# Reordering the start of a diffusion block: the conditions' loads first, weights ahead of w_ada, first products pass by pass

## The chip, the cores and the metric

The kernel runs on one core of a Trainium2 chip. The metric is the device time of one execution in microseconds; lower is better. An execution is some 1.7 us longer than its span, the time from the first to the last of the program's own instructions. Engines are named as in the profile: PE (TensorE), DVE (VectorE), ACT (ScalarE), POOL (GpSimd), SP (SyncE, which here issues the loads).

## What is computed

One block of a hybrid diffusion backbone over 512 latent tokens and 256 context tokens of 1024 features, in fp32. Cut to what bears on the change:

```
mod_lat = split(silu(c) @ w_ada + b_ada, 6)          # scale, shift, gate, twice
mod_ctx = split(silu(c_ctx) @ w_ada + b_ada, 6)
pl = project(modulate(rmsnorm(x, g_mix), sh1, sc1), w_in, w_dec_up, b_dec)
pc = project(modulate(rmsnorm(ctx, g_mix), sh1c, sc1c), w_in, w_dec_up, b_dec)
# project: h @ w_in gives q, k, v, g, dd (decay rank 16, two directions), conv and gate columns;
# dd @ w_dec_up + b_dec -> log decay
o_c, s_cf, s_cb = gla_bidir(context)                  # 4 heads, chunks of 64
o_l = gla_bidir(latent, from the context's states)
...                                                   # short convolution, gates, output projections,
                                                      # SwiGLU, final rmsnorm
```

## The kernel before

A matrix product of two fp32 operands is made from three passes: each operand is split into a rounded high part (fp32r) and the rest, and `mm3` (L153) issues high by high, high by low and low by high into one PSUM bank. A split is one cast on ACT (the high part) and one subtraction on DVE (the low part), `split` at L102 for all tiles.

The start of the program is what the change touches. Four loads bring the 512 latent tokens (`xt`, 128 tokens each), two small ones the conditions c and c_ctx (`c_rows`, 16 rows of 128), then come small vectors. PE turns `c_rows`, ACT takes the SiLU into `c2` and, with a second table, a square root `root`, and then the tokens in turn: `normed` squares and scales a token tile, `turn` transposes it into `xsT` (features on partitions).

The scale and shift of the mixer's input come from the first 2048 columns of w_ada in four parts (`p_` = 0 to 3) of two feature tiles each: `ada_load` issues eight loads of 256 KB a part, `ada_rows` makes 16 matmuls of them, DVE copies the row out (`adar`), `mod_cols` turns it into columns with eight small matmuls (`adac`) and two DVE steps (`modT`, `gs`), and `modulate(f)` makes feature tile f of `h`: ACT writes the high part, DVE scales `xsT` in place and subtracts. Beside each part goes one unit of the projection weights, `w0_load(p_)`: 256 rows of w_in with head 0's value columns, the 32 decay columns and head 0's key and query columns, 544 KB in four loads into one of three buffers `r_w`; `w0_split` splits a unit into `h_w` and `l_w`.

Then a loop over the eight feature tiles k: `gather_v` adds tile k's products to the values and decays of the four latent token tiles (`vo`, four banks, twelve matmuls), `gather_kq` to head 0's keys and queries (`ko`, `qo`, six matmuls). After the odd tiles 1, 3 and 5 the next part follows inside the loop: its w_ada rows, the key and query products of tile k-1, its columns, the first `modulate`, the weights' split, the second `modulate`. After tile 6 the context tokens (normalised after tile 5) are turned and split into `hc`; `head0_gather` then makes the context's products in the same way, and inside it, at k = 5, `ddt` transposes the latent decays (`st` into `ddT`) and `vps2` the late vectors. The context's own decays are turned a little later, behind four steps of the first g tile, and the decays' products `z` follow.

Order: from `pinned[0] = True` (L471) on each engine runs its instructions in the order of the program's text. All loads but those of w_dec_up (POOL) are issued by SP in the order of the text; a load waits there for its buffer, and each load uses one of eight semaphores in turn, so a ninth waits until the first of the eight has landed.

Of the kernel before, what the change touches and what calls it, by code (L numbers as in the profile page):

```python
# [9 lines left out]
F32R = mybir.dt.float32r  # L10
BF16 = mybir.dt.bfloat16
U8 = mybir.dt.uint8
AF = mybir.ActivationFunctionType
ALU = mybir.AluOpType
PSUM = bass.MemoryType.PSUM

P = 128
D = 1024
KT = D // P
T = 512  # L20
TC = 256
NT = T // P
# [24 lines left out]
def hybrid_block(ctx: ExitStack, tc: tile.TileContext, x, c, ctxt, c_ctx, w_ada, b_ada, g_mix, w_in,  # L47
# [8 lines left out]
    wp = ctx.enter_context(tc.tile_pool(name="wp", bufs=3))  # L56
# [8 lines left out]
    def u2(name, dt=F32, shape=(P, 512)):  # L65
        return up.tile(list(shape), dt, tag="u2", name=name, bufs=NU)
# [17 lines left out]
    def bank(name, shape=(P, 512)):  # L84
        return ps.tile(list(shape), F32, tag="ps", name=name, bufs=3)

    def gbank(name, shape=(P, 512)):
        return ps.tile(list(shape), F32, tag="pg", name=name, bufs=5)
# [15 lines left out]
    act_, dve = Pinned(nc.scalar), Pinned(nc.vector)  # L104

    def f32(ap):
        return ap.bitcast(F32)
# [35 lines left out]
    def pe_pin(ins):  # L143
        if pinned[0]:
            tc.keep_in_program_order(ins)

    def mm(*a, **k):
        pe_pin(nc.tensor.matmul(*a, **k))  # L148

    def tr(*a):  # L150
        pe_pin(nc.tensor.transpose(*a))

    def mm3(o, a, b, start, stop):  # L153
        mm(o, a[0], b[0], start=start, stop=False)
        mm(o, a[0], b[1], start=False, stop=False)
        mm(o, a[1], b[0], start=False, stop=stop)

    def rstd_of(ss, n, width, name):

        r = sm.tile([P, n], F32, tag=f"rs{n}", name=f"rs_{name}")  # L160
        act_.activation(r, ss, AF.Sqrt, bias=eps, scale=1.0 / width)
        dve.reciprocal(r, r)
        return r
# [4 lines left out]
    def token_load(i):  # L168
        if i < NT:
            xt = hp.tile([P, D], F32, tag="xt", name=f"xt{i}", bufs=4)  # L170
            nc.sync.dma_start(xt, x[i * P:(i + 1) * P, :])
        else:
            xt = wp.tile([P, D], F32, tag="raw", name=f"xt{i}", bufs=4)
            nc.sync.dma_start(xt, ctxt[(i - NT) * P:(i - NT + 1) * P, :])
        return xt

    xts = [token_load(i) for i in range(NT)]
    c_rows = cst.tile([16, P], F32, name="c_rows")
    nc.sync.dma_start(c_rows[0:8, :], c.rearrange("o (r f) -> (o r) f", f=P))
    nc.sync.dma_start(c_rows[8:16, :], c_ctx.rearrange("(r f) -> r f", f=P))  # L180

    ident = cst.tile([P, P], F32, name="ident")
    make_identity(nc, ident)
# [4 lines left out]
    def small_vectors(vs):  # L188
        for r0, src in vs:
            n = src.shape[1] // P  # L190
            for d in range(src.shape[0]):
                nc.sync.dma_start(vrow[r0 + d * n:r0 + (d + 1) * n, :P], src[d:d + 1, :].rearrange("o (r f) -> (o r) f", f=P))
# [27 lines left out]
    for d in range(2):  # L220
        t = cst.tile([P, NT, P], F32, name=f"TP{d}")
# [21 lines left out]
    xsT = hp.tile([P, KT, T], F32, name="xsT")  # L243

    def normed(i, xt):
        junk = u2(f"junk{i}", BF16, (P, D))
        ss = sm.tile([P, 1], F32, tag="ss", name=f"ss{i}")
        act_.activation(junk, xt, AF.Square, accum_out=ss)
        dve.tensor_scalar_mul(xt, xt, rstd_of(ss, 1, D, f"x{i}"))
# [8 lines left out]
    modT = cst.tile([P, KT, 2, 2], F32, name="modT")  # L258
    gs = cst.tile([P, KT, 2], F32, name="gs")

    def ada_load(p_):

        us = []
        src = w_ada[:, :2 * D].rearrange("(k p) (s f) -> p k s f", p=P, s=2)[:, :, :, p_ * 256:(p_ + 1) * 256]
        if p_ < 2:
            for k in range(0, KT, 2):
                if p_ == 0:
                    t = wp.tile([P, 2, 2, 256], F32, tag="raw", name=f"wa{p_}{k}", bufs=4)
                else:
                    t = hp.tile([P, 2, 2, 256], F32, tag="wa", name=f"wa{p_}{k}", bufs=4)  # L270
                for i in range(2):
                    nc.sync.dma_start(t[:, i], src[:, k + i])
                us += [t[:, i].rearrange("p s f -> p (s f)") for i in range(2)]
        else:
            for k in range(KT):
                t = (uh if p_ == 2 else uo)(f"wa{p_}{k}", F32, (P, 2, 256))
                nc.sync.dma_start(t, src[:, k])
                us.append(t.rearrange("p s f -> p (s f)"))
        return us

    def ada_rows(p_, us):

        rows = gbank(f"ada{p_}")
        for k in range(KT):
            g_ = 32 * (k % 4)
            mm(rows[g_:g_ + 32, :], cw[:, k, :], us[k], start=k < 4, stop=k >= KT - 4)
        rsb = u2(f"adar{p_}")
        dve.tensor_copy(rsb, rows)
        return rsb

    hhi, hlo = hbig("h")
    h = [(hhi[k // 4][:, k % 4, :], hlo[k // 4][:, k % 4, :]) for k in range(KT)]
    hc = []

    def mod_split(src, f, j, hi, lo):
        g_, sh = gs[:, f, j:j + 1], modT[:, f, 0, j:j + 1]
        act_.activation(hi, src, AF.Identity, scale=g_, bias=sh)
        dve.tensor_scalar(src, src, g_, sh, ALU.mult, ALU.add)
        dve.tensor_sub(lo, src, f32(hi))
# [13 lines left out]
    def modulate(f):  # L313
        mod_split(xsT[:, f, :], f, 0, *h[f])
# [34 lines left out]
    def run(steps):  # L349
        for _ in steps:  # L350
            pass
# [83 lines left out]
    NW = HV + 32  # L435

    def w0_load(p_):

        r = hp.tile([P, 2, NW + 256], F32, tag="wr", name=f"r_w0{p_}", bufs=3)
        for d0, c0, n in ((0, CV, HV), (HV, CD, 32), (NW, CK, P), (NW + P, CQ, P)):  # L440
            nc.sync.dma_start(r[:, :, d0:d0 + n], w_in[p_ * 256:(p_ + 1) * 256, c0:c0 + n].rearrange("(a p) b -> p a b", p=P))
        return r

    def w0_at(k, a, e):
        return tuple(w_[:, k % 2, a:e] for w_ in w0[k // 2])

    def gather_v(os, src, k):
        for i, o in enumerate(os):
            mm3(o[:, :NW], tuple(w_[:, i * P:(i + 1) * P] for w_ in src[k]), w0_at(k, 0, NW), k == 0, k == KT - 1)

    def gather(o, c0, src, k, n=T):
# [2 lines left out]
    w0 = []  # L454
# [6 lines left out]
    vo = [bank(f"v0_{NC_}")]  # L461

    wdu_ = wdu_load()
    was, wrs = [], []
    for p_ in range(4):
        was.append(ada_load(p_))
        wrs.append(w0_load(p_))
    small_vectors(((R_GH, g_head), (R_BD, b_dec[0]), (R_WC, w_conv[0])))
    xcs = [token_load(NT + i) for i in range(NC_)]
    lat = (xsT[:, :4, :], xsT[:, 4:, :])  # L470
# [14 lines left out]
    def w0_split(p_):  # L485
        w0.append(split_raw(wrs[p_], f"w0{p_}"))

    modulate(0)
    w0_split(0)
    modulate(1)  # L490
    wdu_split(*wdu_)
    vo += [(bank if i < 3 else gbank)(f"v0_{NC_ + i}") for i in range(1, NT)]
# [11 lines left out]
    for k in range(KT):  # L504
        p_ = k // 2 + 1
        more = k % 2 == 1 and p_ < 4
        gather_v(vo, h, k)
        if more:
            rsb = ada_rows(p_, was[p_])
            gather_kq(k - 1)  # L510
            mod_cols(p_, rsb)
            modulate(2 * p_)
            w0_split(p_)
            modulate(2 * p_ + 1)
            if p_ == 3:
                for i in range(NC_):
                    normed(NT + i, xcs[i])
        if k % 2 or k >= 6:
            gather_kq(k)
        if k == 6:  # L520
            xcT = [wp.tile([P, 4, TC], F32, tag="raw", name=f"xcT{i}", bufs=4) for i in range(2)]
            for i in range(NC_):
                turn(NT + i, xcs[i], xcT, i)
            for f in range(KT):
                mod_ctx(f)
# [12 lines left out]
    def head0_gather():  # L538
        for k in range(KT + 2):
            if k < KT:  # L540
                gather_v(vc, hc, k)
            if k >= 2:
                gather(kc, NW, hc, k - 2, TC)
            if k == 5:
                ddt(NC_, NC_ + NT)
                vps2 = gbank("vps2")
                tr(vps2[:, :R_N], vrow[:R_N, :P], ident[:R_N, :R_N])
                dve.tensor_copy(vec[:, 64:], vps2[:, 64:R_N])
# [370 lines left out]
    for pr in range(KT // 2):  # L919
# [3 lines left out]
        for j in range(2):  # L923
            o = proj(sl_, j, f"cc{pr}{j}")
            t = ux(f"cc{pr}{j}")
# [5 lines left out]
        for j in range(2):  # L931
            ct = 2 * pr + j
            o = proj(sl_, j, f"ch{pr}{j}")
            t = ux(f"u{ct}", F32, (P, ROWS, GW))
# [9 lines left out]
        for j in range(2):  # L944
            o = proj(sl_, j, f"cb{pr}{j}")
            t = ux(f"cbu{pr}{j}")
            nc.vector.tensor_mul(t, o, ucs[j].rearrange("p r w -> p (r w)"))
            hi, lo = ux(f"cuh{pr}{j}", F32R), ux(f"cul{pr}{j}", F32R)
# [13 lines left out]
    for pr in range(KT // 2):  # L962
        ada_tick()
        sl_ = Slab(w_conv_out, pr * 256, 256, f"co{pr}")
        for j in range(2):
            o = proj(sl_, j, f"yc{pr}{j}", rhs=cu)
            nc.vector.tensor_mul(mg[2 * pr + j], o, mg[2 * pr + j])
    oghl = []
    for i, t in enumerate(og):
        mk = uv if i < 3 else ux  # L970
        hi, lo = mk(f"ogh{i}", F32R), mk(f"ogl{i}", F32R)
# [3 lines left out]
    for pr in range(KT // 2):  # L975
        ada_tick()
        sl_ = Slab(w_gla_out, pr * 256, 256, f"go{pr}")
        for j in range(2):
            i = 2 * pr + j
            o = proj(sl_, j, f"yg{pr}{j}", rhs=oghl)  # L980
            t = ux(f"yg{pr}{j}")
            nc.vector.tensor_mul(t, o, sas[pr, j])
            nc.vector.tensor_add(t, t, mg[i])
            hi, lo = ux(f"meh{i}", F32R), ux(f"mel{i}", F32R)
# [105 lines left out]
    for t in range(NT):  # L1090
        o = mix(t, 1, sl_, steps_of(t))
# [12 lines left out]
    for pr in range(FT // 2):  # L1104
# [16 lines left out]
        for j in range(2):  # L1121
# [4 lines left out]
            hi, lo = mk(f"ah{pr}{j}", F32R), mk(f"al{pr}{j}", F32R)  # L1126
# [65 lines left out]
```

## Time and profile before

| what | us |
|---|---|
| three timed runs | 1028.50, 1027.01, 1028.37 |
| their median | 1028.37 |
| the profiled execution | 1028.95 |
| its span | 1027.2 |
| PE busy in it | 992.8 (97%), 5221 matmuls |
| DVE busy | 545.7 (53%) |
| ACT busy | 381.9 (37%) |
[...]
| loads | 114 MB from HBM |

A row of the view in order of time has the start and the duration of one or several equal instructions, the engine, the line, the operation, what it writes and reads, its shape and count; in square brackets how long the engine sat idle before it and what ended that. SPq is a load's issue. Matmuls are pipelined, so that a row of several is shorter than their sum, and the ends are modelled. PEld is the load of stationary weights, which overlaps the matmuls.

### The profile page before, as it was taken

What the parts mean: (1) busy time and instruction counts of PE and PEld (TensorE: products, weight loads), DVE (VectorE), ACT (ScalarE), POOL (GpSimd) and SP (SyncE); (2) the same over time, 40 slices, a digit from 0 to 9 for tenths busy, and PEclk for the clock granted to TensorE, in tenths of its full rate; (3) what the DMA queues carried; (4) which work ended last, traced back from release to release, by engine and by line L of the source; (5) the groups of instructions that cost most, each with busy time, mean ns of one, the idle gap of its engine ahead of it and who ended that gap; (6) DMA issues with size and microseconds to landing.
All of it is one profiled execution on the core that took longest, in us unless ns stands there. A gap on an engine that the chain in (4) does not pass through costs nothing.

```text
span 1027.2 us, 12874 instructions
## 1 busy us (share of the span) xinstructions
PE 992.8 (97%) x5221; PEld 829.6 (81%) x5221; DVE 545.7 (53%) x845; ACT 381.9 (37%) x602; POOL 6.3 (1%) x18
## 2 busy tenths in 40 slices
PE   4888999999999999999999999999999999999997
PEld 2667889888788888888888888888888888888886
DVE  4456868777656587678534434743343333322423
ACT  4146464647635322233213323652332232321323
POOL 2000000000000000000000000000000000000000
PEclk9899999999999999999999999999999999999999
DMA  9714111201245667666632332223233233232302
GB/s 304 245 39 109 59 42 42 60 24 44 80 123 175 204 172 212 192 192 193 212 88 82 104 101 83 83 94 111 82 103 103 82 104 101 83 126 80 123 22 82
DMA packets 109759, 117.16 MB, mean 114 GB/s; under 512 B 5522, under 2 KB 97796, under 8 KB 109700
## 3 DMA queue, kind: packets, MB, share of 16 engines
q1 hardware_dynamic: 109444, 116.07, 37.5%
q8 instruction: 41, 0.67, 0.3%
q0 software_dynamic: 256, 0.26, 0.1%
q14 instruction: 18, 0.15, 0.0%
HBM read 114.22 MB, written 2.10 MB: 113 GB/s over the span
## 4 chain that ended last, share of the span: by engine, by line
PE 91%; DMA 3%; DVE 3%; ACT 2%; SPq 1%; issue 1%; ACTq 0%; DVEq 0%
PE f L148 23%; PE fo L148 10%; PE v L148 6%; PE yc L148 4%; PE yg L148 4%; PE gb L148 4%; PE cb L148 4%; PE g L148 4%; PE cc L148 4%; PE ch L148 4%; PE ga L148 4%; PE mx L148 3%; PE kl L148 2%; PE o L148 2%; PE q L148 2%; PE F L148 2%
## 5 line engine op out<-in xcount | busy, mean ns | idle before, releaser
L148 PE MATMUL f<-h,h_fa 128*128 128x512 f32 (+1 forms) x384 | 111.0, 372 | 0.2 <-DVE h L102 0.2
L148 PE MATMUL f<-h,h_fb 128*128 128x512 f32 (+1 forms) x384 | 110.3, 372 | 0.0
L148 PEld LDWEIGHTS f<-h,h_fa 128*128 128x128 f32 x384 | 70.2, 188 | 13.3 <-DVE h L102 0.8
L148 PEld LDWEIGHTS f<-h,h_fb 128*128 128x128 f32 x384 | 70.0, 188 | 12.5
L148 PE MATMUL f<-h,l_fb 128*128 128x512 f32 (+1 forms) x192 | 71.3, 371 | 0.0
L148 PE MATMUL f<-h,l_fa 128*128 128x512 f32 (+1 forms) x192 | 71.3, 371 | 0.0
L102 DVE TENSOR_TENSOR l_fa<-r_fa,h_fa 128x1024 fp32r<-128x1024 f32 x22 | 26.9, 1225 | 74.6 <-ACT h_fa L102 74.6
L102 DVE TENSOR_TENSOR l_fo<-r_fo,h_fo 128x1024 fp32r<-128x1024 f32 x22 | 26.9, 1224 | 68.7 <-ACT h_fo L102 68.7
L148 PE MATMUL fo<-h_fo,ah 128*128 128x512 f32 x154 | 60.5, 393 | 0.0
L148 PE MATMUL fo<-l_fo,ah 128*128 128x512 f32 x154 | 60.5, 393 | 0.0
L148 PE MATMUL fo<-h_fo,al 128*128 128x512 f32 x154 | 60.4, 392 | 0.0
L909 DVE SCALAR_TENSOR_TENSOR acc<-r_wa,c,acc 128x256 f32<-128x256 f32 x112 | 54.1, 483 | 8.1 <-DMA r_wa<-in_w_ada_dram 5.4
L102 ACT CAST h_fo<-r_fo 128x1024 fp32r<-128x1024 f32 x22 | 23.1, 1050 | 71.0 <-PE fo L148 27.4
L148 PEld LDWEIGHTS f<-h,l_fb 128*128 128x128 f32 x192 | 36.2, 188 | 6.2
L148 PEld LDWEIGHTS f<-h,l_fa 128*128 128x128 f32 x192 | 36.1, 188 | 6.2
L148 PE MATMUL gb<-h,h_gb 128*128 128x512 f32 x128 | 40.0, 394 | 0.0
L148 PE MATMUL g<-h,h_g 128*128 128x512 f32 x128 | 39.8, 392 | 0.0
L148 PE MATMUL cb<-h,h_cb 128*128 128x512 f32 x128 | 39.7, 391 | 0.0
L148 PE MATMUL ch<-h,h_ch 128*128 128x512 f32 x128 | 39.6, 390 | 0.0
L148 PE MATMUL cc<-h,h_cc 128*128 128x512 f32 x128 | 39.6, 390 | 0.0
L148 PE MATMUL ga<-h,h_ga 128*128 128x512 f32 x128 | 39.4, 390 | 0.0
L148 PE MATMUL v<-h_v,h 128*128 128x256 f32 x192 | 36.3, 285 | 0.0
(298 smaller groups left out, 2270.8 us busy)
## 6 DMA issues: line engine op xcount, KB each, us to landing
r_wa<-in_w_ada_dram SPq DMA_DIRECT2D x32, 512.0 KB, 4.2
r_fa<-in_w_ffn_in_dram SPq DMA_DIRECT2D x22, 512.0 KB, 3.5
r_fb<-in_w_ffn_in_dram SPq DMA_DIRECT2D x22, 512.0 KB
r_fo<-in_w_ffn_out_dram SPq DMA_DIRECT2D x22, 512.0 KB, 3.5
wa<-in_w_ada_dram SPq DMA_DIRECT2D x32, 256.0 KB, 5.4
r_g<-in_w_in_dram SPq DMA_DIRECT2D x8, 512.0 KB, 4.0
r_gb<-in_w_in_dram SPq DMA_DIRECT2D x8, 512.0 KB
r_cc<-in_w_in_dram SPq DMA_DIRECT2D x8, 512.0 KB, 3.9
```

Of the source, the lines that this page charges most:

```text
L102: return lambda *a, **k: pin(getattr(self.engine, op)(*a, **k))
L148: pe_pin(nc.tensor.matmul(*a, **k))
L909: nc.vector.scalar_tensor_tensor(acc, w_[:, k, :], ck, acc, ALU.mult, ALU.add)
```

## The change

The loads of c and c_ctx are issued ahead of the four token loads. From part 1 on a part's weight unit is loaded ahead of its w_ada tiles, and its split stands at the head of the part, ahead of the odd tile's products. Of these, the first two token tiles' stay ahead of the part's w_ada rows, the other two move behind both `modulate` steps. In part 0 the weights' cast stands ahead of the first `modulate` on ACT, and its subtraction between the two DVE steps of feature tile 0. Tile 0's twelve products go pass by pass over the four banks rather than bank by bank. The transposes of the latent decays and of the late vectors go from k = 5 to k = 7 of the context's loop.

```diff
--- before.py
+++ after.py
@@ -174,10 +174,10 @@
             nc.sync.dma_start(xt, ctxt[(i - NT) * P:(i - NT + 1) * P, :])
         return xt
 
-    xts = [token_load(i) for i in range(NT)]
     c_rows = cst.tile([16, P], F32, name="c_rows")
     nc.sync.dma_start(c_rows[0:8, :], c.rearrange("o (r f) -> (o r) f", f=P))
     nc.sync.dma_start(c_rows[8:16, :], c_ctx.rearrange("(r f) -> r f", f=P))
+    xts = [token_load(i) for i in range(NT)]
 
     ident = cst.tile([P, P], F32, name="ident")
     make_identity(nc, ident)
@@ -444,8 +444,15 @@
     def w0_at(k, a, e):
         return tuple(w_[:, k % 2, a:e] for w_ in w0[k // 2])
 
-    def gather_v(os, src, k):
-        for i, o in enumerate(os):
+    def gather_v(os, src, k, passes=False, base=0):
+        if passes:
+
+            for a, b in ((0, 0), (0, 1), (1, 0)):
+                for i, o in enumerate(os, base):
+                    mm(o[:, :NW], src[k][a][:, i * P:(i + 1) * P], w0_at(k, 0, NW)[b],
+                       start=k == 0 and a + b == 0, stop=k == KT - 1 and a == 1)
+            return
+        for i, o in enumerate(os, base):
             mm3(o[:, :NW], tuple(w_[:, i * P:(i + 1) * P] for w_ in src[k]), w0_at(k, 0, NW), k == 0, k == KT - 1)
 
     def gather(o, c0, src, k, n=T):
@@ -463,8 +470,11 @@
     wdu_ = wdu_load()
     was, wrs = [], []
     for p_ in range(4):
+        if p_:
+            wrs.append(w0_load(p_))
         was.append(ada_load(p_))
-        wrs.append(w0_load(p_))
+        if p_ == 0:
+            wrs.append(w0_load(p_))
     small_vectors(((R_GH, g_head), (R_BD, b_dec[0]), (R_WC, w_conv[0])))
     xcs = [token_load(NT + i) for i in range(NC_)]
     lat = (xsT[:, :4, :], xsT[:, 4:, :])
@@ -485,8 +495,21 @@
     def w0_split(p_):
         w0.append(split_raw(wrs[p_], f"w0{p_}"))
 
-    modulate(0)
-    w0_split(0)
+    def mod_lo(f):
+        g_, sh = gs[:, f, 0:1], modT[:, f, 0, 0:1]
+        src = xsT[:, f, :]
+        dve.tensor_scalar(src, src, g_, sh, ALU.mult, ALU.add)
+        yield
+        dve.tensor_sub(h[f][1], src, f32(h[f][0]))
+
+
+    w0.append(tuple(wp.tile([P, 2, NW + 256], F32R, tag=t, name=f"{t}_w00", bufs=4) for t in ("whi", "wlo")))
+    act_.copy(w0[0][0], wrs[0])
+    act_.activation(h[0][0], xsT[:, 0, :], AF.Identity, scale=gs[:, 0, 0:1], bias=modT[:, 0, 0, 0:1])
+    lo = mod_lo(0)
+    next(lo)
+    dve.tensor_sub(w0[0][1], wrs[0], f32(w0[0][0]))
+    run(lo)
     modulate(1)
     wdu_split(*wdu_)
     vo += [(bank if i < 3 else gbank)(f"v0_{NC_ + i}") for i in range(1, NT)]
@@ -504,17 +527,20 @@
     for k in range(KT):
         p_ = k // 2 + 1
         more = k % 2 == 1 and p_ < 4
-        gather_v(vo, h, k)
         if more:
+            w0_split(p_)
+            gather_v(vo[:2], h, k)
             rsb = ada_rows(p_, was[p_])
             gather_kq(k - 1)
             mod_cols(p_, rsb)
             modulate(2 * p_)
-            w0_split(p_)
             modulate(2 * p_ + 1)
+            gather_v(vo[2:], h, k, base=2)
             if p_ == 3:
                 for i in range(NC_):
                     normed(NT + i, xcs[i])
+        else:
+            gather_v(vo, h, k, passes=k == 0)
         if k % 2 or k >= 6:
             gather_kq(k)
         if k == 6:
@@ -541,7 +567,7 @@
                 gather_v(vc, hc, k)
             if k >= 2:
                 gather(kc, NW, hc, k - 2, TC)
-            if k == 5:
+            if k == KT - 1:
                 ddt(NC_, NC_ + NT)
                 vps2 = gbank("vps2")
                 tr(vps2[:, :R_N], vrow[:R_N, :P], ident[:R_N, :R_N])
```

## Rows read from the trace of the kernel before

**Rows 1.** Busy time by stretch: stretch, us, each engine (instructions), PE clock, DMA share, GB/s.

```profile
0.00:92.30 92.30, 66.24 (x388) 51.40 (x388) 48.55 (x111) 35.55 (x70) 6.27 (x18) 0.94 0.62 185
92.30:1027.20 934.90, 926.51 (x4833) 778.19 (x4833) 497.14 (x734) 346.34 (x532) 0.00 (x0) 1.00 0.36 107
10.00:40.00 30.00, 22.63 (x127) 15.98 (x127) 15.04 (x31) 13.03 (x24) 0.00 (x0) 0.94 1.11 334
29.60:33.00 3.40, 3.40 (x16) 3.40 (x16) 3.29 (x7) 0.00 (x0) 0.00 (x0) 0.50 1.13 330
67.10:70.50 3.40, 3.40 (x14) 3.01 (x13) 2.15 (x5) 1.20 (x3) 0.00 (x0) 0.50 0.01 2
```

**Rows 2.** In order of time: the conditions' transpose, first token's square, part 0's w_ada.

```profile
9.74 0.25 PE L226 MATMUL cps<-ident,c_rows 16*128 16x16 f32 x1 [9.74 <-DMA c_rows<-in_c_ctx_dram]
...
11.73 1.04 ACT L102 ACTIVATE junk<-xt 128x1024 bf16<-128x1024 f32 x1
...
21.52 1.92 PE L148 MATMUL ada<-wa,cw 128*32 128x512 f32 x16
```

**Rows 3.** One load each: issue (ns, start) and time to landing.

```profile
L171 SPq DMA_DIRECT2D xt<-in_x_dram x1: 392/392/392, 0.8 to 0.8; - x1
...
DMA to landing us min/median/max: 3.8/3.8/3.8
...
L272 SPq DMA_DIRECT2D wa<-in_w_ada_dram x1: 467/467/467, 11.6 to 11.6; - x1
...
DMA to landing us min/median/max: 5.1/5.1/5.1
...
L441 SPq DMA_DIRECT2D r_w<-in_w_in_dram x1: 368/368/368, 38.6 to 38.6; - x1
...
DMA to landing us min/median/max: 4.5/4.5/4.5
```

**Rows 4.** In order of time: part 0's scale, cast and split; part 1's w_ada.

```profile
25.94 0.81 ACT L102 ACTIVATE h<-xsT,modT,gs 128x512 fp32r<-128x512 f32 x1 [4.37 <-DVE gs L102]
26.66 1.08 ACT L102 CAST h_w<-r_w 128x1088 fp32r<-128x1088 f32 x1
...
27.98 1.29 DVE L102 TENSOR_TENSOR l_w<-r_w,h_w 128x1088 fp32r<-128x1088 f32 x1
...
34.10 1.92 PE L148 MATMUL ada<-wa,cw 128*32 128x512 f32 x16
```

**Rows 5.** In order of time: part 2's w_ada to part 3's.

```profile
46.99 1.92 PE L148 MATMUL ada<-wa,cw 128*32 128x512 f32 x16
...
50.33 0.95 PE L148 MATMUL adac<-sel,adar 128*128 128x2 f32 x8
...
51.72 0.82 ACT L102 ACTIVATE h<-xsT,modT,gs 128x512 fp32r<-128x512 f32 x1 [10.36 <-DVE gs L102]
...
53.15 0.69 DVE L102 TENSOR_TENSOR h<-xsT,h 128x512 fp32r<-128x512 f32 x1
...
53.57 0.40 PE L148 MATMUL v<-h_w,h 128*128 128x288 f32 x1 [0.78 <-ACT h_w L102]
...
55.10 0.40 PE L148 MATMUL v<-l_w,h 128*128 128x288 f32 x1 [1.13 <-DVE l_w L102]
...
58.34 1.92 PE L148 MATMUL ada<-wa,cw 128*32 128x512 f32 x16
```

**Rows 6.** In order of time: the context's turn.

```profile
70.95 1.04 PE L151 MATMUL xtp<-ident,xt 128*128 128x128 f32 x8
```

**Rows 7.** In order of time: the decays' turns and what lies between them.

```profile
85.83 0.30 PE L151 MATMUL ddt<-ident,st 128*128 128x128 f32 x1 [0.92 <-ACT st L102]
...
86.88 2.35 DVE L102 TENSOR_TENSOR l_g<-r_g,h_g 128x1024 fp32r<-128x1024 f32 x2
...
91.04 0.24 ACT L102 COPY st<-ddh 128x64 f32<-128x64 f32 x1
...
91.42 0.38 PE L151 MATMUL ddt<-ident,st 128*128 128x128 f32 x2
```

## The prediction

> **What bounds the kernel now.** I read the busy times by stretch first [rows 1]. After 92.3 us the TensorE (PE) is busy 926.51 of 934.90 us at full clock: a shift that reaches that point reaches the end, and nothing later can give much back. In the first 92.3 us PE is busy only 66.24; 26 us are idle, and the change touches nothing but this stretch. [...] (1) Until 21.5 us the chain begins at the load of the conditions: their transpose waits until 9.74 us for c_ctx, which stands behind the four token loads; only then come c's SiLU, a table load and, at 11.73, the first token's square; the four tokens run 9.8 us from there to w_ada's first part at 21.52 [rows 2]. The first token had landed at 0.8 + 3.8 = 4.6 us [rows 3]. (2) From 21.5 to 71 us the chain is PE's own order: w_ada rows of a part, columns, scale and shift, split, products, next part. The loads run ahead: the queue moves 334 GB/s between 10 and 40 us [rows 1], w_ada's part 0 is complete at 11.6 + 5.1 = 16.7, the last unit of weights at 38.6 + 4.5 = 43.1 [rows 3], while part 3's w_ada is wanted only at 58.34 [rows 5]. (3) From about 74 us to 91 VectorE (DVE) sets the pace with the context's split and head 0's values (part 5 below). [...]
>
> The sum is made against the profiled execution, 1028.95 us (span 1027.2), which lies 0.6 above the median of the three timed runs, 1028.37.
>
> **1. Conditions first.** SP issues two 4 KB loads (0.39 us for an issue like it [rows 3]) ahead of the tokens: everything behind lands up to 0.8 us later; I take 0.8 all along. No row shows a small load on an empty queue. Upper bound: as long as the 512 KB token at the head, 3.8 us [rows 3]; lower: that less its 512 KB at 334 GB/s [rows 1], 3.8 - 1.6 = 2.2. So c_ctx, issued at 1.2, lands at 3.4 to 5.0; I take 3.4, since 4 KB carries no data time. Transpose to first square is 11.73 - 9.74 = 2.0 [rows 2]: square at 5.4 to 7.0, and token 0 is there at 4.6 + 0.8 = 5.4. Plus 9.8: PE ready for w_ada at 15.2 to 16.8, against 21.52. Here the next limit comes: part 0 lands at 16.7 + 0.8 = 17.5, and its last eighth is used 1.5 us into the 1.92 us stretch, so this starts in effect at 16.0. Gain 21.52 - 16.0 = 5.5 (bounds 4.7 and 6.3).
>
> [...]
>
> **2. First products.** ScalarE (ACT) starts part 0's first scale 25.94 - 21.52 = 4.4 after w_ada begins [rows 2, 4], now 20.4. The cast of the weights (1.08 [rows 4]) stands ahead of it on ACT: an added wait, with both scales and so all first products queued behind it. Its 0.53 MiB follow part 0 on the queue. From 16.7 to 43.1 the queue brought three w_ada parts and four weight units, 8.1 MiB, 3.25 us per MiB [rows 3]: landed at 19.2, cast done at 20.3, hidden; were the load 1 us later, it costs 0.9. Then DVE does scale 0, l_w (1.28 [rows 4]), low part 0, and both steps of feature 1. Scale start to low part's end is 53.84 - 51.72 = 2.12, the low part itself 0.69 [rows 5], so feature 1's low part ends at 20.4 + 1.43 + 1.3 + 0.7 + 1.3 = 25.1. Pass by pass, tile 0's twelve products are done by then; of tile 1 only half (six products) stands ahead of w_ada, and five of these wait for that low part or what is behind it. At the low clock (16 products in 3.4 us [rows 1], 0.21 each) that is 25.1 + 1.1 + 0.2 for the issue = 26.4 for w_ada's part 1; 6.0 after the scale, 8.16 now [rows 4]: gain 2.1. Part 1 has landed at 17.5 + 3.06 x 3.25 = 27.5, and less 1.5 this is 26.0: just in time. What is late next: part 1's l_w and then the copy of w_ada's rows stand on DVE behind the splits of w_dec_up; DVE is full, 3.29 of 3.40 us, where these run now [rows 1]. 25.1 + 2.7 + 1.3 = 29.1, while the copy would otherwise start near 28.5; products of k and q cover most of that. Loss 0.2 (bounds 0 and 0.6).
>
> **3. A part's period.** In part 2, at full clock, w_ada to w_ada is 58.34 - 46.99 = 11.35; part 1 has 12.89 with a low stretch [rows 4, 5]. PE idles 0.78 for the cast and 1.13 for l_w [rows 5]. Both go: the split is now made a part ahead, in ACT's and DVE's spare time. In their place PE waits on the scale alone, and half the products (six) plus k and q stand over it. New period: to the end of the columns 51.28 - 46.99, 4.2 with the overlap of the next weight load; six products 0.8 (24 take 3.24 from 55.10 [rows 5]); k and q 1.4 (48.91 to 50.33 [rows 5]); low part ready at 46.99 + 6.85, so a stall of 0.3; twelve products 1.65; six 0.8; issue 0.2: 9.3. Gains 12.89 - 9.3 = 3.6 and 11.35 - 9.3 = 2.05. Loads: part 2 at 17.5 + 5.6 x 3.25 = 35.7, part 3 at 17.5 + 8.1 x 3.25 = 43.9; less 1.5, 34.2 and 42.4 against starts at 26.4 + 0.2 + 9.3 = 35.9 and 45.2. Spare 1.7 and 2.8. The fourth weight unit is moved past part 3 on SP's queue and needs unit 0's buffer, free when l_w ends near 23; the queue comes to it near 30. Cost nothing; if the buffer were late, part 3 and the context tokens would stand behind it.
>
> **4. To the context's turn.** Now 70.95 - 58.34 = 12.6 [rows 5, 6], with a low stretch from 67.1 [rows 1]. After: 4.2 + 0.8 + 1.4 + 0.3 + 1.65 + 1.4 = 9.75. Gain 2.85. The context tokens, 1 MiB behind part 3, land near 48; ACT comes to them at 45.2 + 4.7 + 1.7 = 51.6.
>
> **5. Latent decays' turn two steps later.** It removes three stalls of PE on ACT's st, the last 0.92 [rows 7], by 2.3 us of products now put ahead. But DVE's order stays: ddT, l_g (2.35), the context's values, st at 91.04 to 91.28, and the context's own turn at 91.42 without a wait [rows 7]. PE comes there earlier and waits for the same st. Gain 0.1; upper bound the whole 2.0, lower -1.7 (one more low stretch of 3.4 us at half speed, if idle time gathers there).
>
> **Sum.** 5.5 + 2.1 - 0.2 + 3.6 + 2.05 + 2.85 + 0.1 = 16.0; from 1028.95 this is 1012.9, from the median 1012.4. I predict 1012.5.
>
> **Rivals.** (a) The load queue becomes the bound. Two weight units in a row are eight issues that carry 1.06 MiB; SP takes about 0.5 us for one (467 ns [rows 3]), 4.1 us in all against 3.4 of data. For it: part 1 has only 0.4 us to spare. Against: the queue is some 5 us ahead (5.1 from issue to landing [rows 3]). Losing 3 us eats the spare and costs 1 to 2.6: 1013.5 to 1015.5. (b) The clock. PE now waits for part 0's loads with less work behind it, and low stretches follow waits: one beside each of two parts costs 1.7 each (half of 3.4 [rows 1]): 1014 to 1017. [...] (c) The conditions do not come sooner, because what holds the first square is another thing: 1012.5 + 5 = 1017.5; against it speaks the wait's own row [rows 2]. [...] (e) No change: the time saved is given back at 92 us by the loads of head 1; against, only 0.36 of the queue is in use there [rows 1].
>
> **How the numbers follow.** Forecast 0.62 (1010.5 to 1014.5 with the bounds of parts 1, 2 and 5), (a) 0.14, (b) 0.14, (c) 0.05, (d) 0.03, (e) 0.02. The range leaves out (c), (d), (e) and the far ends of the others: 1009.8 to 1016.8. About 0.2% (2 us) is what a measurement can tell from no change. Faster 0.95, same 0.02, slower 0.03.
>
> **What would show it.** In the trace of after: first square at 5.4 and w_ada's part 0 ending near 17.9 behind its load (part 1); first scale near 20.4, part 1's w_ada at 26.4 (part 2); the next at 35.9 and 45.2, with no PE wait for a cast or l_w between (part 3); the context's turn near 54.9 (part 4); PE waiting over 1 us for st ahead of the context's own turn, and z near 76 instead of 92.3 (part 5). The prediction is wrong if w_ada's starts follow their landings, if low stretches come in parts 2 and 3, or if z's shift is not the end's.

## The result and the profile after

| | before | after |
|---|---|---|
| median of four runs, us | 1028.43 (1027.01 to 1028.85) | 1014.03 (1012.52 to 1014.11) |
| profiled execution, us | 1028.95, span 1027.2 | 1013.98, span 1012.3 |
| mean granted clock in the profile | 0.993 | 0.997 |
| the context's turn begins, us | 70.95 | 54.38 |
| head 0's z begins, us | 92.31 | 75.66 |
| first score products begin, us | 116.17 | 101.17 |

After takes 0.9859 of the time before, 95% interval 0.9842 to 0.9876: 14.4 us less, where the prediction said 15.9 (1012.5 from 1028.37). Three of the four runs lie at 1014.0 to 1014.1 with a mean clock of 0.996 or 0.997; the fourth is at 1012.52 with 0.999.

The busy times by stretch, cut at z as in [rows 1] (stretch, us, each engine with instructions, PE clock, DMA share, GB/s):

```profile
0.00:75.65 75.65, 62.25 (x387) 47.00 (x388) 48.78 (x111) 35.64 (x70) 6.41 (x18) 1.00 0.75 225
75.65:1012.30 936.65, 927.70 (x4830) 779.31 (x4833) 496.96 (x734) 346.35 (x532) 0.00 (x0) 1.00 0.35 107
10.00:40.00 30.00, 27.36 (x169) 17.72 (x169) 18.22 (x34) 10.05 (x16) 0.00 (x0) 1.00 1.12 327
77.10:80.60 3.50, 3.50 (x10) 2.71 (x9) 3.03 (x4) 3.47 (x6) 0.00 (x0) 0.51 0.00 1
```

The first row is 16.65 us shorter than its counterpart, the second 1.75 us longer: 934.90 before, 936.65 now. Up to z the clock is 1.00 throughout, where it was 0.94. PE's idle time there falls from 26.06 to 13.40 us, and its busy time from 66.24 to 62.25: almost the same instructions, none of them at the low clock. Behind z stands the low stretch of the last row, 3.4 us at half of the full clock (0.51 over the row's 3.50); before had 1.00 there.

The rows that answer to [rows 2] and [rows 4], in order of time:

```profile
2.69 0.25 PE L226 MATMUL cps<-ident,c_rows 16*128 16x16 f32 x1 [2.69 <-DMA c_rows<-in_c_ctx_dram]
...
5.33 1.06 ACT L102 ACTIVATE junk<-xt 128x1024 bf16<-128x1024 f32 x1 [0.57 <-DMA xt<-in_x_dram]
...
15.20 2.88 PE L148 MATMUL ada<-wa,cw 128*32 128x512 f32 x16
...
17.03 0.14 PEld L148 LDWEIGHTS ada<-wa,cw 128*32 128x32 f32 x2 [0.60 <-DMA wa<-in_w_ada_dram]
...
20.47 1.52 ACT L102 ACTIVATE h<-xsT,modT,gs 128x512 fp32r<-128x512 f32 x2 [0.40 <-DVE gs L102]
...
23.12 0.79 PE L148 MATMUL v<-wlo_w,h 128*128 128x288 f32 x4 [0.99 <-DVE wlo_w L102]
...
25.64 2.22 PE L148 MATMUL ada<-wa,cw 128*32 128x512 f32 x16
...
27.50 1.29 DVE L102 TENSOR_TENSOR l_w<-r_w,h_w 128x1088 fp32r<-128x1088 f32 x1
...
28.71 0.68 DVE L102 COPY adar<-ada 128x512 f32<-128x512 f32 x1
...
29.44 0.97 PEld L148 LDWEIGHTS adac<-sel,adar 128*128 128x128 f32 x8 [0.44 <-DVE adar L102]
```

What ends last changes hands four times in 30 us: the conditions until 2.69, the first token at 5.33, part 0's w_ada load at 17.03 (the stretch takes 2.88 us instead of 1.92, for the wait of 0.60 in its last eighth), and then the low part of the first weights at 23.12. At 28.71 the copy of w_ada's rows stands behind l_w on DVE, and PE waits 0.44 for it.

The rest of the parts and the decays' turns, against [rows 5] to [rows 7]:

```profile
35.43 1.92 PE L148 MATMUL ada<-wa,cw 128*32 128x512 f32 x16
...
42.34 0.30 PEld L148 LDWEIGHTS v<-h_w,h 128*128 128x128 f32 x2 [0.31 <-DVE h L102]
...
44.65 1.92 PE L148 MATMUL ada<-wa,cw 128*32 128x512 f32 x16
...
54.38 1.03 PE L151 MATMUL xtp<-ident,xt 128*128 128x128 f32 x8
...
69.26 0.30 PE L151 MATMUL ddt<-ident,st 128*128 128x128 f32 x1 [0.61 <-ACT st L102]
...
71.58 0.50 PE L148 MATMUL g<-h,l_g 128*128 128x512 f32 x1 [0.40 <-DVE l_g L102]
...
74.84 0.30 PE L151 MATMUL ddt<-ident,st 128*128 128x128 f32 x1 [0.92 <-ACT st L102]
75.66 0.62 PE L148 MATMUL z<-ddT,wdu 64*128 64x256 f32 x4 [0.52 <-DVE ddT L102]
...
77.01 0.95 PE L148 MATMUL g<-h,h_g 128*128 128x512 f32 x2
...
82.05 0.62 PE L148 MATMUL g<-h,h_g 128*128 128x512 f32 x2
...
101.17 0.31 PE L148 MATMUL F<-q,k 128*32 128x64 f32 x8
```

In before the last two instants, z and the first score products, were these:

```profile
92.31 0.62 PE L148 MATMUL z<-ddT,wdu 64*128 64x256 f32 x4 [0.52 <-DVE ddT L102]
...
116.17 0.31 PE L148 MATMUL F<-q,k 128*32 128x64 f32 x8
```

No row of parts 1 to 3 waits for a cast or for l_w any more. What is left of waits gathers at the end: 0.61 for the latent decays' st, 0.40 for l_g, 0.92 for the context's st and 0.52 for ddT. Right behind, the same two products that take 0.62 us at 82.05 take 0.95 at 77.01: that is the low stretch as PE's rows show it.

### The profile page after: what moved, and what is told of

Its sections match the earlier page's. It is cut to its first block, busy times and chain, and to the rows that moved or that the text cites. A ratio compares the mean times of both kernels' runs of the same rounds, so it can differ in the third digit from the quotient of the medians.

```text
span 1012.3 us, 12874 instructions
## 1 busy us (share of the span) xinstructions
PE 989.9 (98%) x5217; PEld 826.3 (82%) x5221; DVE 545.7 (54%) x845; ACT 382.0 (38%) x602; POOL 6.4 (1%) x18
## 4 chain that ended last, share of the span: by engine, by line
PE 91%; DVE 4%; ACT 3%; issue 1%; DMA 1%; SPq 0%; ACTq 0%; DVEq 0%
PE f L148 24%; PE fo L148 11%; PE yc L148 4%; PE yg L148 4%; PE gb L148 4%; PE cb L148 4%; PE cc L148 4%; PE ch L148 4%; PE ga L148 4%; PE g L148 4%; PE v L148 4%; PE mx L148 3%; PE kl L148 2%; PE o L148 2%; PE q L148 2%; PE F L148 2%
## 5 line engine op out<-in xcount | busy, mean ns | idle before, releaser
L1150 DVE TENSOR_TENSOR sil<-sil,f 128x512 f32<-128x512 f32 x22 | 15.1, 687 | 39.7 <-PE f L148 39.7
```

Source lines behind the costliest of these rows:

```text
L1150: nc.vector.tensor_mul(sil, sil, obs[2 + j])
```

## The experiments

One table holds the instants of all profiled executions, since nearly every verdict is read from them. z and F are the starts of head 0's z and of the first score products; "rest" is the span less F's start. (The expectations of e3 and e4 count to the 32 products behind F, at 102.01 in after, and so from z some 0.84 us more.) A ratio below is to the runs of before in the same session, with its 95% interval in brackets. The medians of before lay between 1027.18 and 1028.59, so that the medians of two kernels from different sessions carry about as much doubt; the traces say more.

| kernel | w_ada of parts 0 to 3 | turn | z | z to F | rest | low stretch behind the turn | median us |
|---|---|---|---|---|---|---|---|
| before | 21.52, 34.10, 46.99, 58.34 | 70.95 | 92.31 | 23.86 | 911.03 | none | 1028.43 |
| after | 15.20, 25.64, 35.43, 44.65 | 54.38 | 75.66 | 25.51 | 911.13 | 77.1 | 1014.03 |
| e1_cond_only | 15.07, 28.74, 40.10, 52.99 | 65.50 | 86.97 | 23.86 | 911.07 | none | 1023.53 |
| e2_no_cond | 21.22, 30.81, 40.60, 49.84 | 59.56 | 80.84 | 25.45 | 911.11 | 82.0 | 1017.79 |
| e3_ddt_back | as after, within 0.4 | 54.76 | 78.62 | 23.88 | 911.10 | 68.8, twice as long | 1014.71 |
| e4_more_g | as after, within 0.1 | 54.47 | 75.87 | 21.82 | 913.31 | 100.4 | 1012.77 |
| e5_dummy | as after, within 0.1 | 54.30 | 76.30 | 23.87 | 911.03 | none | 1013.13 |
| e6_ada_first | 15.38, 26.15, 36.37, 45.59 | 55.31 | 76.59 | 25.45 | 911.06 | 77.1 | 1014.78 |
| e7_no_half | 15.05, 26.54, 36.56, 46.57 | 56.29 | 77.57 | 23.87 | 911.06 | none | 1014.29 |
| e8_late_split | 15.13, 25.76, 36.65, 47.21 | 58.26 | 79.53 | 23.90 | 911.07 | none | 1016.33 |
| e9_no_passes | 15.45, 26.23, 35.62, 44.84 | 54.56 | 75.85 | 25.45 | 911.10 | 76.6 | 1014.10 |
| e10_fill_all | as after, within 0.2 | 54.57 | 75.95 | 23.26 | 913.69 | 103.6, twice as long | 1013.87 |

The last columns are the cleanest reading of this study. From z to F a kernel takes 23.9 us, or 25.5 where a low stretch lies there; from F to the end all but e4 and e10, which move real work ahead of F, take 911.0 to 911.1. So for these z's instant and one stretch of clock account for the whole time of the profiled execution.

The instants themselves shift with the start. The first scale begins at 20.47 us in after, and between 20.40 and 20.99 in e3 to e10, though none of their edits reaches back to it. From the first scale to z after takes 55.19, e2 55.20 and e9 55.18. So an edit behind the first scale is priced below by that stretch, and not by z alone.

**Conditions alone, and everything but the conditions.**

```diff
-    xts = [token_load(i) for i in range(NT)]
     c_rows = cst.tile([16, P], F32, name="c_rows")
     nc.sync.dma_start(c_rows[0:8, :], c.rearrange("o (r f) -> (o r) f", f=P))
     nc.sync.dma_start(c_rows[8:16, :], c_ctx.rearrange("(r f) -> r f", f=P))
+    xts = [token_load(i) for i in range(NT)]
```

That is e1_cond_only, made on the kernel before; e2_no_cond is the reverse, made on after.

> The kernel before with the conditions' loads first, and nothing else of the change. Theory (limits in turn, each stretch of the start worth its own sum): first square at 5.3 instead of 11.73, part 0's w_ada ends near 18 behind its load, first scale near 20.4 instead of 25.94, and the 5.5 us carry to the end: part 1's w_ada near 28.6, z near 86.8, time 1028.4 - 5.5 = 1022.9, give or take 1.7 for a low clock stretch more or less. Rival (the conditions pay only together with the weights ahead, because the load queue or the split then holds the parts): z moves by less than 3 us, time 1025.5 or more.

> The changed kernel with the conditions' loads behind the tokens again. Theory: first square back at 11.7, first scale at 25.9; from there each stretch as in the changed kernel (part 1's w_ada 5.2 after the scale, 9.2 to 9.8 a part, 9.7 to the context's turn), so z near 81.1 and the time 1014.0 + 5.4 = 1019.4, or 1.7 less without the low stretch. Rival (stretches overlap: with a later start the loads are further ahead and the parts run faster): z nearer than 4 us to the changed kernel's 75.66, time under 1018.

In e1 the first square begins at 5.26, the first scale at 20.59, and z is 5.34 us earlier than before: near the 5.5 that the prediction's part 1 gave the edit. The median falls by less, 1027.18 (before, on the same chip) to 1023.53, ratio 0.9958 [0.9945, 0.9971]. The runs' mean clock tells why: before's at 1026.9 to 1027.7 have 0.995, e1's median run 0.993; e1's fastest, with 0.995, is at 1022.24, 4.7 below before's at that clock. In e2 the first square is back at 11.43 and z at 80.84, 5.18 later than after; the ratio to before is 0.9903 [0.9886, 0.9920], the median 3.8 above after's. The profiled run, at 1019.10, has the low stretch and lies 5.1 above after's; the other three, at 1017.51 to 1017.98, lie 1.1 to 1.6 lower, as if without it. The conditions are worth 5.2 to 5.3 us at z, with or without the other edits.

**The weights' split.** e8_late_split puts the split between the part's two scale-and-shift steps:

```diff
-            w0_split(p_)
             gather_v(vo[:2], h, k)
...
             modulate(2 * p_)
+            w0_split(p_)
             modulate(2 * p_ + 1)
```

> The changed kernel with the weights' split between the two scale steps again, as before the change; the loads stay ahead, the products stay halved. Theory (the cast and l_w then stand between scale and first product): w_ada to w_ada 10.6 to 10.8 instead of 9.2, PE waiting about 1.3 us for l_w in each part, z 4.0 to 4.5 later, near 80, time 1018. Rival (halving the products already covers it): z within 1.5 us, time 1015.5 or less.

The period of a part is 10.9 and 10.6 us instead of 9.8 and 9.2, and PE waits for l_w again; the waits between 13 and 58 us (us in total, times, longest):

```profile
PE v L148 <- DVE l_w L102: 3.4, 3, 1.1
PE v L148 <- DVE wlo_w L102: 1.0, 1, 1.0
```

z is 3.9 us later than after, 3.7 counted from the first scale (58.93 instead of 55.19). The median is 1016.33, 0.9884 [0.9867, 0.9900], only 2.3 above after's, since no low stretch follows z (z to F 23.90). Making the split ahead of w_ada is worth 3.7 us at z.

**Half of the products behind w_ada.** e7_no_half puts all twelve ahead of it:

```diff
-            gather_v(vo[:2], h, k)
+            gather_v(vo, h, k)
...
-            gather_v(vo[2:], h, k, base=2)
```

> The changed kernel with all twelve products of tiles 1, 3 and 5 ahead of the part's w_ada, none behind both scale steps. Theory (in the parts PE waits only for the scale and its low part, and six products cover 0.8 us of that): w_ada to w_ada 10.0 to 10.1 instead of 9.2, z 2.4 later than 75.66, at 78.0, time 1016.4, less 1.7 without a low stretch. Rival (k and q alone cover the wait): z within 0.5 us, time as the changed kernel.

The period is 10.0 us, and PE waits for the scale's low part at three parts, on which the kept half lay as a cover:

```profile
PE v L148 <- DVE h L102: 2.3, 3, 0.8
```

z comes at 77.57, 1.9 later than after (1.8 from the first scale), and yet the median is 1014.29, 0.9863 [0.9846, 0.9879], beside after's 1014.03. The table shows where the 1.9 went: no low stretch follows, and z to F takes 23.87 instead of 25.51. The waits ahead of z are all there, and behind them the clock is full:

```profile
76.75 0.30 PE L151 MATMUL ddt<-ident,st 128*128 128x128 f32 x1 [0.93 <-ACT st L102]
77.57 0.62 PE L148 MATMUL z<-ddT,wdu 64*128 64x256 f32 x4 [0.52 <-DVE ddT L102]
...
77.50:84.00 6.50, 6.43 (x30) 5.19 (x31) 4.12 (x7) 5.98 (x9) 0.00 (x0) 1.00 0.26 52
```

**The order of the loads, and the passes.** e6_ada_first loads each later part's w_ada ahead of its weights, as before did; e9_no_passes takes the first tile's products bank by bank.

```diff
-        if p_:
-            wrs.append(w0_load(p_))
         was.append(ada_load(p_))
-        if p_ == 0:
-            wrs.append(w0_load(p_))
+        wrs.append(w0_load(p_))
```

```diff
-            gather_v(vo, h, k, passes=k == 0)
+            gather_v(vo, h, k, passes=False)
```

> The changed kernel with the loads of parts 1 to 3 in the old order, w_ada's tiles ahead of the part's weights; the splits stay early. Theory (the loads run some parts ahead, so their order matters only in part 1): the cast of part 1's weights waits for its load until about 26 to 27, l_w and the copy of the w_ada row behind it end up to 1 us later, z 0 to 0.9 later than 75.66, time 1014.0 to 1014.9 with a low stretch after z. Rival (weights ahead in the queue are what makes the early split possible): every part waits for its weights, z 3 us later or more.

> The changed kernel with tile 0's twelve products bank by bank. Theory (the second and third product then wait for l_w and for the low part, ten products follow instead of four, but w_ada's part 1 and its copy are held by their load and by DVE's work of w_dec_up): w_ada's part 1 starts 0.3 to 0.5 later, its row's copy and z not at all, z at 75.7, time 1014.0, or 1012.5 without the low stretch. Rival (PE's first products are on the path): z 0.4 or more later.

In e6 the cast of the second weights waits for its load, and the columns for the copy that is late behind it:

```profile
27.31 1.10 ACT L102 CAST h_w<-r_w 128x1088 fp32r<-128x1088 f32 x1 [4.79 <-DMA r_w<-in_w_in_dram]
...
30.39 1.05 PE L148 MATMUL adac<-sel,adar 128*128 128x2 f32 x8 [0.74 <-DVE adar L102]
```

z is 0.9 later, but 0.5 of that is there at the first scale already (20.99 against 20.47), which this edit does not reach; e1, with the old order too, has it at 20.59. From the first scale to z it is 55.60 instead of 55.19: the order of the loads is worth 0.4 at z. The median is 1014.78, 0.9864 [0.9848, 0.9880]. In e9 z is 0.2 later, but so is the first scale (20.67 against 20.47) and this edit does not reach back to that; PE's wait for the low part of the first weights grows from 0.99 to 1.4 and is given back. The median is 1014.10, 0.9858 [0.9844, 0.9873]: the passes are worth nothing that shows.

**The latent decays' turn.**

```diff
-            if k == KT - 1:
+            if k == 5:
```

> The changed kernel with the latent decays' turn at k = 5 again. Theory A (the turn's place gains 0.1 at z and nothing else, but the low clock stretch after z comes from the idle time that it gathers ahead of the context's turn): context's turn at 54.4 as in the changed kernel, z at 75.7 to 75.8, no low stretch behind z, z to the first score products 24.7 as in the kernel before instead of 26.35, time 1012.5. Rival B (the low stretch falls by chance of the moment, whatever the turn's place): times spread over the same two levels, 1012.5 and 1014.0, median like the changed kernel's. Rival C (the later turn does save its stalls): z at 77 or later, time 1015 or more.

In the profiled execution the three stalls are back (0.67, 0.92 and 0.93 us), and the low clock falls among these rather than behind z:

```profile
68.80:75.60 6.80, 5.96 (x26) 5.83 (x27) 4.60 (x10) 3.61 (x10) 0.00 (x0) 0.50 0.34 94
```

z comes at 78.62, 3.0 later than after (0.4 of it there at the first scale), and z to F is 23.88. For this execution theory A was wrong: the earlier place had a low stretch too. But before has stalls of the same lengths at that place (0.68, 0.93 and 0.92), and there the clock stayed full behind them:

```profile
86.20:92.30 6.10, 5.60 (x36) 4.93 (x36) 4.66 (x9) 3.18 (x9) 0.00 (x0) 1.00 0.49 136
```

The four runs took 1012.36, 1014.10, 1015.33 and 1015.46 us with clocks of 0.998 to 0.995, median 1014.71, 0.987 [0.9851, 0.9889], no difference from after that these runs can tell. This spread over several levels is what rival B expected: whether a low stretch follows the waits seems to differ from run to run of one kernel, and what decides it stays open.

**Dummy products in the wait.** e5_dummy adds ten products of zeros ahead of the context's turn, whose result nobody reads:

```diff
     fill(4, -1)
+    idle = bank("idle")
+    for _ in range(10):
+        mm(idle, zeros[:, :P], zeros, start=True, stop=True)
     ddt(0, NC_)
```

> The changed kernel with ten matmuls of zeros, whose result nobody reads, on PE between the fourth step of the first g tile and the context's decays' turn, where it waits for st. Theory (the low clock stretch after z, 1.65 us, follows from that idle time): no low stretch between 60 and 95 us, z at 75.7 to 76.2 (ten take 2.2 us against 1.5 of wait), z to the first score products 23.9 instead of 25.5, time 1012.5 to 1013, tight. Rival (the low stretch has another cause, earlier work or the moment): low stretch after z as before, time 1014 or more.

The stretch that was low in after, in e5:

```profile
77.10:80.60 3.50, 3.50 (x16) 2.86 (x16) 3.20 (x5) 3.48 (x6) 0.00 (x0) 1.00 0.00 0
```

Sixteen products in 3.5 us instead of ten, clock 1.00. z is 0.64 later, because the zeros run a little over the time that they were to fill, and z to F is 23.87: 1.64 back. The median is 1013.13, 0.9854 [0.9837, 0.9872], 0.9 below after's, where 1.64 - 0.64 says 1.0, though the intervals of the two ratios overlap. That fits a low stretch that comes of PE's waits ahead of z, but it does not show it: with the waits left as they are, e6 has the low stretch and e7 has none (both wait 0.16, 0.93 and 0.52), nor has e8 (0.92 and 0.51). So its absence in e5 could be the moment's doing as well. What the profiles show is the other half: each low stretch in the table, and each of before's three ahead of z, begins during a wait of PE or at most 1.5 us behind the end of one (waits of 0.52 to 1.7 us).

**Real work in the wait.** e4_more_g moves three of the pending g steps ahead of z, two of them into the wait ahead of the context's turn; e10_fill_all is e4 with four more steps moved ahead of the first scores.

```diff
-    SPLITS0 = (5, 9)
+    SPLITS0 = (8, 9)
...
-    fill(4, -1)
+    fill(6, -1)
     ddt(0, NC_)
+    fill(1, -1)
...
-    fill(5, -1)
+    fill(2, -1)
```

```diff
-    ORDER0 = "17 B 3 B 4 B 6 B 9 B 1 F0 5 B 1 kt0 1 A 4 F1 kv0 4 kt1 1 A 1 A 2 kv1 3 A 3 o 8 A 13 ot"
+    ORDER0 = "17 B 3 B 4 B 6 B 9 B 5 F0 1 B 1 kt0 1 A 4 F1 kv0 4 kt1 1 A 1 A 2 kv1 3 A 3 o 8 A 13 ot"
```

> The changed kernel with six steps of the first g tile ahead of the context's decays' turn instead of four, one more between turn and z, and the weights' splits at the same places between them. Theory (PE idles 1.5 to 1.6 us for st there and 0.5 for ddT, and the work that follows is PE's): z some 0.7 later, near 76.4, no PE wait for st above 0.2, the first score products 1.3 us earlier than 102.0 with a low stretch and 3 us earlier without; time 1012.7 with and 1011.0 without. Rival (z sets the pace through the decays on ScalarE and VectorE): first score products at 102.0 or later, time 1014 or more.

> The kernel with six steps of g ahead of the context's turn and one behind it, and in addition the first head's first score products four steps of v later, where PE waited 1.47 us for the scaled keys. Theory (PE's idle time is the loss, and each low clock stretch follows one): no PE wait above 0.6 us between 72 and 105, no low stretch there, the work after the score products 1.4 us earlier than in the kernel with more g alone and 1.7 more where the low stretch goes: time 1009.5. Rival (the wait only moves to the next thing that needs the scaled keys, kt0 or the second direction's score products): time 1012 or more.

e4 has no low stretch behind z and comes to F 3.5 us before after does: 1.64 from the clock, 2.05 from the steps that are done by then, less 0.21 for a later z. There it waits for the scaled keys, and the clock falls there instead:

```profile
99.47 2.25 PE L148 MATMUL F<-q,k 128*64 128x64 f32 x32 [1.47 <-DVE k L102]
...
100.40:103.90 3.50, 3.50 (x30) 3.03 (x23) 3.50 (x9) 0.37 (x1) 0.00 (x0) 0.51 0.69 202
```

The wait is 0.53 in after. From F the span is 913.31 instead of 911.13, so 2.2 of the 3.5 are given back; the median is 1012.77, 0.9855 [0.9840, 0.9870]. In e10 the wait has only moved on, to the transposes of the scaled keys:

```profile
PE kt L151 <- DVE k L102: 1.7, 1, 1.7
```

A low stretch of 6.8 us begins in it; 1013.87, 0.9857 [0.9835, 0.9878]. In both kernels the chain of work that ended last runs from z to the scaled keys on ACT and DVE alone, and the first of these are done at 99.42 us in e4 and at 99.49 in e10, with four more steps on PE ahead. So this chain is the next bound, and more work put ahead of it on PE does not bring it forward.

**Both.** e11_more_g_warm is e4 with the fill of the first score bank with zeros repeated, which leaves the result as it is:

```diff
-        mm(F.rearrange("p s c -> p (s c)"), zeros[:, :P], zeros, start=True, stop=True)
+        for _ in range(8 if (hd, d) == (0, 0) else 1):
+            mm(F.rearrange("p s c -> p (s c)"), zeros[:, :P], zeros, start=True, stop=True)
```

> The kernel with more of g ahead of the context's turn (1012.77) with the zero fill of the first score bank made eight times instead of once, so that PE works through most of its 1.47 us wait for the scaled keys; the result is the same. Theory (there the low stretch at 100.4 follows the wait): no low stretch between 70 and 140 us, first score products at the same time within 0.3, time 1011.0 to 1011.3. Rival (the low stretch comes from work before that, or moves on): 1012.6 or more.

Three runs at 1011.42 to 1011.48 and one at 1013.84; median 1011.48, 0.9840 [0.9825, 0.9855]. It is 2.5 us below after's median and 17 below before's, the fastest version here, though its interval and after's overlap. The profiled execution is the run at 1013.84, in which the tokens' stage is late (w_ada's part 0 at 16.43), so its instants are not in the table; what it shows is the place of the repair:

```profile
100.00:104.00 4.00, 4.00 (x51) 2.33 (x50) 4.00 (x7) 1.69 (x4) 0.00 (x0) 1.00 0.48 135
```

PE is busy throughout and the clock is whole where e4's was 0.51. From z (78.29) to its end that run takes 933.81 us, e4 935.13: 1.3 less, as the medians say (1012.77 and 1011.48). Its instants are 2.4 us later than e4's, so its clock alone could be the moment's doing, as in e5; that three runs lie 1.3 below all four of e4 (1012.71 to 1012.79) speaks for the fill.

## Why the prediction was right, step by step

**What bounds the kernel** held: a shift that reaches z reaches the end, within 0.1 us from F on in ten kernels. What did not hold is that nothing behind z could give anything back; 1.65 us between z and F did, and that belongs to part 5.

**Part 1** said first square 5.4, w_ada done at 17.9 behind its load, first scale 20.4, a gain of 5.5. Measured: 5.33, 18.08, 20.47, 5.47. c_ctx came earlier than the lower bound (landed by 2.69, against 3.4), and that was worth nothing, since the first token and then part 0's load end last, as the step said. e1 and e2 give the edit 5.3 and 5.2.

**Part 2** said w_ada's part 1 at 26.4 and a late copy of 0.2. Measured 25.64, with 0.44 of PE's wait for the copy. The 0.8 us: feature 1's low part ends at 24.85 (24.16 and 0.69) instead of 25.1, and the five products behind it and the issue take 0.79 instead of 1.3, for they run at full clock, where the step had carried over the low one of before.

**Part 3** said a period of 9.3, with a stall of 0.3 on the low part. Measured 9.79, which holds the late copy and part 1's wait for its load, and 9.22, with a wait of 0.31 at 42.34. From the first scale to z the change gains 11.2 us (66.37 before, 55.19 after). The edits in that stretch are now priced apart: the early split 3.7, the halved products 1.8, the load order 0.4, the passes nothing. Each was undone alone, so the other 5.2 is argued, not shown: three low stretches of before lie ahead of z and none of after's, and three times half of 3.4 is 5.1. PE's busy time up to z, 4.0 less for almost the same instructions, speaks for it. What keeps the clock up is not isolated: e8 has its waits for l_w back, up to 1.1 long, and no low stretch ahead of z.

**Part 4** said 9.75 and the turn at 54.9. Measured 9.73 and 54.38. Up to here the sum said 15.9, the trace says 16.57.

**Part 5** is the term that was mis-sized. It said 0.1, between 2.0 and -1.7. At z it is 16.65 - 16.57 = 0.1; but the waits that it foresaw ahead of the context's turn (0.92 and 0.52 measured) are followed by the low stretch of its lower bound, and z to F takes 1.65 more. In e5, with most of that idle time filled, the 1.64 are back; e3 shows no gain for the old place. The bound did not have to come: e7 and e8 have the waits and not the stretch, and the four runs of after seem to divide three to one. But it was likely enough to carry weight in the sum: the prediction had itself written that idle time gathers there and that low stretches follow waits, in rival (b), and put it on the loads of the parts.

**The sum**, then: 0.7 more than said from parts 2 and 3, 1.7 less from part 5, so 15.0 instead of 16.0 between the profiled executions (1028.95 to 1013.98). Of the 1.5 by which 1012.5 was missed, that is 1.0; the other 0.5 is the base, since before's profiled execution lies 0.5 above its median and after's does not. That parts 2 and 3 made good a part of what part 5 lost is luck. The run at 1012.52, with a mean clock of 0.999, fits the case without that stretch; it has no trace that would show it.

**The rivals.** (a) is there only at part 1, where 0.3 us of its w_ada is a wait for the load (2.22 instead of 1.92). (b) named what came, a low stretch behind waits, at the wrong place. (c) and (e) did not come: the square followed the conditions (2.0 us behind their transpose before, 2.6 after, the last 0.57 a wait for the token), and the loads of head 1 cost nothing (911.13 from F to the end, 911.03 before). The clock was full, 1.00, through all parts.

## What to carry to other kernels

Ask of a wait not only how long it is but whether the clock falls behind it: here 1.44 us of waits (0.92 and 0.52) were followed by a loss of 1.65 more, in some kernels and runs and not in others. So the range for an edit that ends in PE waiting at a new place should hold a low stretch there. Fill such a wait with pending work as far as the next chain allows, and what is left of it with products of zeros (1.3 us from e4 to e11). Compare runs by their mean granted clock before a difference of 1.5 us is put down to an edit, and read stretches of the trace from one instant to another behind the edit: those agreed to 0.1 us, where the instants themselves moved with the start by up to 0.6 and single runs spread by 1.5.

## What the runs showed of the hardware

A load of 4 KB, issued by SP at 1.26 us behind one other of 4 KB, had landed when its reader started at 2.69: 1.4 us at most. The prediction's lower estimate was 2.2, worked out from the 512 KB load of a token (3.8 us from issue to landing) less 1.6 for its bytes at 334 GB/s. The measurement is below it.

A low stretch of the table was 3.4 us long, in e3 and e10 6.8, with a granted clock of 0.50 or 0.51 where a window was laid over it (after, e2, e3, e4, e9). Each lies at a wait or close behind one: in before the three ahead of z begin at 29.6, 43.2 and 67.1, that is 0.3, 1.0 and 0.7 us behind waits of 1.12, 1.13 and 1.13, in after 1.5 behind one of 0.52. But a wait does not always bring one. In before itself PE waits 0.78 for the cast and 1.13 for l_w in each of parts 1 to 3, and a low stretch follows in parts 1 and 3 and none in part 2; e6 and e7 differ in the same way behind waits of the same lengths (0.16, 0.93 and 0.52). What differs between them besides the instants is not known.
